# The first norm of a two-block transformer kernel: its loads get places of their own, and its script goes by quarters

## The chip, the cores and the metric

The kernel runs on one core of one Trainium2 chip. The metric is the device time of one execution in microseconds (us); lower is better.

## The reference

Two transformer blocks run one after the other on 256 tokens of 1024 features. The change touches only the beginning of the first block: the modulation vector from the condition `c`, the first norm with its shift and scale, and the first columns of the input projection that follow it.

```python
def first_block(x, c, w_ada, b_ada, norm1_pre, ...):
    ada = jax.nn.silu(c) @ w_ada[l] + b_ada[l]            # 6 x 1024 values
    sh1, sc1, g1, sh2, sc2, g2 = jnp.split(ada, 6, axis=-1)
    h = modulate(rms_norm(x, norm1_pre[l]), sh1, sc1)     # norm * (1 + sc1) + sh1
    y = token_mixer(h, w_in[l], ...)                      # begins with h @ w_in
    x = x + g1[:, None, :] * rms_norm(y, norm1_post[l])
    ...                                                   # expert layer, second block
```

## The kernel before

Activations lie with features on the 128 partitions: 1024 features are eight groups (k = 0 to 7) of 128 rows by 256 tokens. Weights come in slabs of 128 by 1024 float32 (512 KB, one load each). Each projection slab is split into a high part (`whi`, ScalarE, line 315) and a low part (`wlo`, VectorE or, for a few listed slabs, GpSimd, line 323), and the activations likewise (`h[0]`, `h[1]`); a product of a slab and a feature group is three matmuls, high by high, high by low, low by high (lines 404 to 406). Slabs 3 and 4 of `w_qk` are among those whose low part GpSimd makes.

The start of `mixer` follows two lists that were written by hand. Every engine works through its own instructions in the order in which the program issues them, and all loads of this part are issued by SyncE, in one queue.

`LOADS` is the order of the loads. `x0`, `x1` are the two halves of the input; `w1` to `w5` the first five slabs of `w_qk`; `S0` to `S7` the eight slabs of `w_sh`, which hold the columns of `w_ada` for the shift; `c0` to `c7` the eight slabs of `w_ada` for the scale, transposed. The slabs S and c go through `pieces`: `ask` issues their loads into tiles of a pool (here `mraw`, four buffers), `piece` takes the next one and computes with it.

`START` is the order of the work. A name that is in `LOADS` means: take all pieces up to this one. For S that is four matmuls into one row of 256 values, eight instructions in the trace (`shift`, line 746): two S slabs give 256 shift values, a quarter of the features. For c it is a dot product on VectorE with the row `crow`, the condition on all partitions (`dot`, lines 522 and 523). The other names are steps: `q` squares of half the input and their column sums (lines 778 and 571), `R` the reciprocal root, `B` its spread over the partitions (line 576), `X` a quarter of the normed input (line 789), `H` the transposes that turn a quarter of the shift from a row into columns (lines 793 to 797), `u` the use of the next weight slab, with its split, `h` and `l` the modulated feature group and its split (lines 818, 681, 683, 400), `P` all products that have become possible and are not done.

`crow` is made on TensorE: eight broadcasts of the condition's columns (line 576), and two copies by ScalarE (line 765). The tiles of the pool `sp` (the pool `mix`) have one buffer for each tag: a tile that names a tag takes over the buffer of the earlier tile of that tag.

When the script is done, the kernel loads five more weight slabs, appends the other 32 units of the modulation to `pieces` (they are taken one at a time during the following projections), and goes on with `w_if`, the rest of `w_qk`, `w_v` and so on.

Of the kernel before, what the change touches and what calls it, by code (L numbers as in the profile page):

```python
# [11 lines left out]
F32 = mybir.dt.float32  # L12
# [5 lines left out]
AF = mybir.ActivationFunctionType  # L18
# [3 lines left out]
P = 128  # L22
T = 256
D = 1024
KC = 8
# [4 lines left out]

START_SLABS = 5
START_LOADS = 4
LOADS = (
    "S0 x0 x1 S1 S2 w1 S3 S4 w2 w3 S5 w4 w5 S6 c0 S7 c1 c2 c3 c4 c5 c6 c7"
).split()
START = (
    "S0 q0 q1 S1 H0 R0 S2 B0 X0 X1 X2 X3 S3 u0 S4 u1 S5 u2 H2 u3 P0 H1 S6 c0 h0 S7 c1 l0 u4 H3 h1 c2 l1 "
    "h2 P1 c3 l2 h3 P2 c4 l3 h4 c5 l4 P3 P4 h5 c6 l5 P5 h6 c7 l6 P6 h7 l7 P7"  # L40
).split()

POOL_FFN = [5, 7, 9]
# [7 lines left out]
OFF, HALF = 4, 8  # L51
# [83 lines left out]
def _outsT(w):  # L135

    return np.ascontiguousarray(w.T).reshape(-1, P, D)
# [8 lines left out]
def _layout(i):  # L146
    o = {}
    o["cols"], offs = _cols(i)
    o["xT"] = np.ascontiguousarray(i["x"][0].T.reshape(KC, P, T).transpose(1, 0, 2))
    o["crow"] = np.ascontiguousarray(i["c_2"])  # L150
    o["posr"] = np.ascontiguousarray(i["positions_2"].reshape(1, T))
    o["posc"] = np.ascontiguousarray(i["positions_2"].reshape(2, P).T)
    w = i["w_ada"][0]
    o["w_sh"] = np.ascontiguousarray(w[:, :D].reshape(2, 4, P, 4, T).transpose(3, 0, 2, 1, 4)).reshape(-1, P, D)
    o["w_ada"] = _outsT(w[:, D:])
    w = i["w_in"][0]
    o["w_c"], o["w_b"], o["w_x"] = (_blocksT(w[:, j * D:(j + 1) * D]) for j in range(3))
    o["w_qk"] = _blocksT(w[:, 3 * D:4 * D])
# [28 lines left out]
    r = uq[:, :, 128:]  # L187
# [80 lines left out]
class Body:  # L268
# [236 lines left out]
    def crow_of(self, pool):  # L505

        c = pool.tile([P, D], F32, name="crow1")
        self.nc.sync.dma_start(c, self.a["crow"].broadcast_to([P, D]))
        return c

    def silu_row(self, c, e):
# [125 lines left out]
        self.nc.sync.dma_start(self.x[:, s], self.a["xT"][:, s])  # L637

    def ada_u(self, units):
        self.add_cols(lambda u: self.a["w_ada"][u - KC], self.ada, self.colr("b_ada", 0, 48), units)  # L640

    def mod_u(self, l, units):
        self.add_cols(lambda u: self.a[f"mod{l}"][u - (ROW_UNITS if l == 0 else 0)], self.mod[l], self.colr("mod_b", 48 * l, 48), units)
# [77 lines left out]
    def mixer(self):  # L721
        nc, a = self.nc, self.a
        with ExitStack() as ctx:
            self.tmps = ctx.enter_context(self.pool_l("tmps1", 14))
            sp = ctx.enter_context(self.pool_l("mix", 1))
            self.mctx = ExitStack()
            mp = self.mctx.enter_context(self.pool_r("mraw", 4))
# [3 lines left out]
            x = self.x  # L731

            c8 = self.cp.tile([P, KC], F32, name="c8")
# [5 lines left out]
            def shift(n):  # L739
                q, b = divmod(n, 2)  # L740

                def take(raw):
                    if b == 0:
                        v[q] = self.pst()
                    for k in range(4):
                        nc.tensor.matmul(v[q][0:1, :T], c8[:, 4 * b + k:4 * b + k + 1], raw[:, k * T:(k + 1) * T],
                                         start=b == 0 and k == 0, stop=b == 1 and k == 3)
                return take

            for w in LOADS:  # L750
                n = int(w[1])
                if w[0] == "S":
                    self.pieces.append((a["w_sh"][n], shift(n)))
                elif w[0] == "c":
                    self.ada_u([KC + n])
                else:
                    self.pieces.append(({"x": lambda n=n: self.load_x(n), "w": lambda n=n: self.load(n)}[w[0]], None))
            self.cap, self.hold = START_SLABS, 1
            self.pieces_in(mp, START_LOADS)
            self.crow = sp.tile([P, D], F32, name="crow0")  # L760
            for n in range(2):
                pt = self.pst()
                for k in range(4):
                    self.bcast(pt[:, k * P:(k + 1) * P], c8[:, 4 * n + k:4 * n + k + 1])
                nc.scalar.activation(self.crow[:, n * 512:(n + 1) * 512], pt, AF.Copy)
            st = self.pst()
            xn = f8("xn", "qk")
            a1 = self.cp.tile([P, KC], F32, name="a1")
            h = act8("h")
# [1 line left out]
            pair = [sp.tile([P, 2 * D + HALF], F32R, name="w3" + m, tag="ya" + m)[:, :2 * D].rearrange("p (a t) -> p a t", t=D) for m in "hl"]  # L771
            for n in range(3, START_SLABS):
                self.spare[n] = [t[:, n - 3] for t in pair]

            def sums(n):
                for kc in range(4 * n, 4 * n + 4):
                    sq = self.tmp("sq")
                    nc.scalar.activation(sq, x[:, kc], AF.Square)
                    self.colstat(st, sq, 0, kc == 0)
# [37 lines left out]
            def high(k):  # L817
# [4 lines left out]
                         u=lambda j: ws.append(self.use(("w_qk", j, 0, D))))  # L822
            left = list(LOADS)
            for w in START:
                if w in left:
                    n = left.index(w) + 1
# [4 lines left out]
            self.cap = 9999  # L831
            self.load(START_SLABS + self.RAW)
            self.ada_u(range(16, 48))
            self.hold = 0


            qk = f8("qk")
# [23 lines left out]
            self.after()  # L861
            for j in range(START_SLABS):
                self.spawn(g_qk(pts[j]))
# [49 lines left out]

            for j in range(START_SLABS, 8):
                self.block("w_qk", j, h, g_qk)
# [3 lines left out]
            vs = sp.tile([P, 2, D], F32, name="vs")  # L919
# [3 lines left out]
            so = f8("so")  # L923
# [9 lines left out]
            hm = f8("hm")  # L933
# [102 lines left out]
            sga, sgm = f8("sga"), f8("sgm")  # L1036
# [39 lines left out]
            st = self.pst()  # L1076
# [1001 lines left out]
```

## Time and profile before

| what | value |
|---|---|
| median of 3 runs | 1741.29 us (1740.84 to 1745.04) |
| profiled execution | 1745.1 us, its span in the trace 1743.0 us |
| TensorE busy | 1710.9 us, 98% of the span |
| VectorE, ScalarE, GpSimd busy | 1381.6, 1037.9, 218.1 us |
| bytes moved | 371.17 MB, 213 GB/s on average |

The span is the time from the first to the last instruction of the profiled execution; the device time of the same execution has 2.1 us around it. Busy times of TensorE count matmuls that run into each other, and "granted clock" (PEclk) is the clock of TensorE as a share of 2.4 GHz.

### The profile page before, as it was taken

The page shows a single profiled execution, that of the slowest core. Times are in us where ns is not written, and L with a number is a line of the kernel's source. Part 1 is how long each engine was busy: PE and PEld are TensorE (multiplying, and loading weights), DVE is VectorE, ACT ScalarE, POOL GpSimd, SP SyncE. Part 2 cuts the span into 40 slices and gives each one's busy share as a digit, 9 for nine tenths or more (in the row PEclk, how much of TensorE's full clock was granted, in tenths as well). Part 3 has the DMA queues.
Part 4 walks back from the last instruction along what each step waited for, and adds up shares of the span by engine and source line. Part 5 has one row for each costly group of instructions (what it writes and reads, how often), then busy time and mean ns, then how long its engine had stood idle before and what let it go on. Part 6 is the DMA issues. An engine that isn't in the chain of part 4 may idle for free.

```text
span 1743.0 us, 33343 instructions
## 1 busy us (share of the span) xinstructions
PE 1710.9 (98%) x12720; PEld 1594.2 (91%) x12720; DVE 1381.6 (79%) x2845; ACT 1037.9 (60%) x1910; POOL 218.1 (13%) x235
## 2 busy tenths in 40 slices
PE   8999999999999999999999999999999999999997
PEld 5899999799999999998888888888999998999997
DVE  4778778589988889987878888876799867688754
ACT  3764544455555999975544555555676547567543
POOL 1110100000010876540000000030200000020001
PEclk8999999999999999999999999999999999999999
DMA  8676677555555544447888888852367664436562
GB/s 291 249 255 217 218 255 248 187 170 182 194 182 183 165 162 159 161 155 276 301 312 297 291 304 299 291 187 98 126 233 289 235 254 159 156 123 217 183 182 72
DMA packets 102400, 371.17 MB, mean 213 GB/s; under 512 B 11456, under 2 KB 11968, under 8 KB 101856
## 3 DMA queue, kind: packets, MB, share of 16 engines
q1 hardware_dynamic: 101664, 365.76, 61.2%
q0 software_dynamic: 576, 3.29, 0.5%
q8 instruction: 99, 1.62, 0.4%
q14 instruction: 61, 0.50, 0.1%
HBM read 365.99 MB, written 2.10 MB: 211 GB/s over the span
## 4 chain that ended last, share of the span: by engine, by line
PE 88%; DVE 4%; ACT 3%; DMA 2%; issue 2%; POOL 1%; POOLq 0%; ACTq 0%; DVEq 0%; SPq 0%
PE ps L404 20%; PE ps L406 19%; PE ps L405 19%; PE ps L1282 5%; PE ps L1281 5%; PE ps L1283 5%; DMA wraw<-v 2%; PE ps L1210 2%; PE ps L571 1%; DVE wlo L323 1%; PE ps L451 1%; PE ps L452 1%; PE ps L453 1%; PE ps L476 1%; PE ps L478 1%
## 5 line engine op out<-in xcount | busy, mean ns | idle before, releaser
L315 ACT ACTIVATE whi<-wraw 128x1024 fp32r<-128x1024 f32 (+1 forms) x548 | 574.1, 1050 | 450.4 <-PE ps L405 191.7
L323 DVE TENSOR_TENSOR wlo<-wraw,whi 128x1024 fp32r<-128x1024 f32 (+1 forms) x538 | 650.0, 1212 | 51.2 <-ACT whi L315 50.0
L404 PE MATMUL ps<-h2h,whi 128*128 128x256 f32 x1152 | 329.8, 286 | 0.0
L406 PE MATMUL ps<-h2h,wlo 128*128 128x256 f32 x1152 | 320.4, 278 | 0.2 <-DVE wlo L323 0.2
L405 PE MATMUL ps<-h2l,whi 128*128 128x256 f32 x1152 | 317.4, 276 | 0.0
L406 PE MATMUL ps<-hhh,wlo 128*128 128x256 f32 x800 | 224.5, 281 | 4.2 <-DVE wlo L323 4.2
L404 PE MATMUL ps<-hhh,whi 128*128 128x256 f32 x800 | 227.4, 284 | 0.9 <-ACT hhh L683 0.8
L405 PE MATMUL ps<-hhl,whi 128*128 128x256 f32 x800 | 224.2, 280 | 1.3 <-DVE hhl L400 1.1
L404 PEld LDWEIGHTS ps<-h2h,whi 128*128 128x128 f32 x1152 | 216.4, 188 | 0.4 <-ACT za L681 0.4
L405 PEld LDWEIGHTS ps<-h2l,whi 128*128 128x128 f32 x1152 | 216.7, 188 | 0.0
L406 PEld LDWEIGHTS ps<-h2h,wlo 128*128 128x128 f32 x1152 | 215.5, 187 | 0.6 <-DVE wlo L323 0.4
L1282 PE MATMUL ps<-whi,al 128*128 128x512 f32 x512 | 199.9, 390 | 0.8 <-DVE al L400 0.8
L1281 PE MATMUL ps<-whi,ah 128*128 128x512 f32 x512 | 199.5, 390 | 0.5 <-ACT ah L1227 0.4
L1283 PE MATMUL ps<-wlo,ah 128*128 128x512 f32 x512 | 199.2, 389 | 0.0
L1202 POOL TENSOR_SCALAR L<-iota,i1T,eT 128x128 bf16<-128x128 f32 x128 | 143.1, 1125 | 270.1 <-DVE mT L1504 136.9
L522 DVE SCALAR_TENSOR_TENSOR mraw<-mraw,crow 128x1024 f32<-128x1024 f32 x128 | 157.1, 1227 | 0.0
L406 PEld LDWEIGHTS ps<-hhh,wlo 128*128 128x128 f32 x800 | 150.1, 188 | 4.8 <-DVE wlo L323 4.8
L404 PEld LDWEIGHTS ps<-hhh,whi 128*128 128x128 f32 x800 | 151.3, 189 | 2.4 <-ACT hhh L683 1.6
L405 PEld LDWEIGHTS ps<-hhl,whi 128*128 128x128 f32 x800 | 150.4, 188 | 2.7 <-DVE hhl L400 2.4
L404 PE MATMUL ps<-hh,whi 128*128 128x256 f32 (+1 forms) x440 | 126.3, 287 | 0.0
L406 PE MATMUL ps<-hh,wlo 128*128 128x256 f32 (+1 forms) x440 | 123.5, 281 | 0.5 <-DVE wlo L323 0.5
L405 PE MATMUL ps<-hl,whi 128*128 128x256 f32 (+1 forms) x440 | 123.0, 279 | 0.0
(461 smaller groups left out, 3509.0 us busy)
## 6 DMA issues: line engine op xcount, KB each, us to landing
wraw<-u SPq DMA_DIRECT2D x128, 512.0 KB, 3.3
wraw<-v SPq DMA_DIRECT2D x128, 512.0 KB, 5.9
mraw<-mod SPq DMA_DIRECT2D x88, 512.0 KB, 4.2
wraw<-fa SPq DMA_DIRECT2D x44, 512.0 KB, 4.2
wraw<-fb SPq DMA_DIRECT2D x44, 512.0 KB, 4.4
mraw<-w_ada SPq DMA_DIRECT2D x40, 512.0 KB, 4.0
wraw<-fo SPq DMA_DIRECT2D x32, 512.0 KB, 4.4
wraw<-wq SPq DMA_DIRECT2D x16, 512.0 KB, 3.6
```

Source lines behind the costliest of these rows:

```text
L315: nc.scalar.activation(t[:, :hi - lo], self.raws[self.n_hi][:, :hi - lo], AF.Copy)
L323: e.tensor_tensor(t[:, :n], self.raws[self.n_lo][:, :n], self.his[self.n_lo].bitcast(F32)[:, :n], ALU.subtract)
L404: mm(out, lh, rh, start=start, stop=False, **kw)
L405: mm(out, lh, rl, start=False, stop=False, **kw)
L406: mm(out, ll, rh, start=False, stop=stop, **kw)
L451: mm(pts[tt][hf], ah, wh[:, s], start=kc == 0, stop=False)
L522: nc.vector.scalar_tensor_tensor(raw, raw, 1.0, self.crow, op0=ALU.mult, op1=ALU.mult, accum_out=acc)
L1202: nc.gpsimd.tensor_scalar(L[:, k], iota, i1, e, op0=ALU.is_equal, op1=ALU.mult)
L1210: nc.tensor.matmul(pg[:, k * P:(k + 1) * P], L[:, k], half[:, k, h], start=h == 1, stop=h == 0)
L1281: mm(o, ah, w[0][:, s], start=first, stop=False)
L1282: mm(o, al, w[0][:, s], start=False, stop=False)
L1283: mm(o, ah, w[1][:, s], start=False, stop=last)
```

## The change

The condition's row is loaded from HBM (`crow0`, to all partitions) and its sigmoid product made there by ScalarE and VectorE; the broadcasts on TensorE go. Of the shift, features 0 to 5 stay with TensorE (six slabs S); features 6 and 7 become dot products like the scale (`s6`, `s7`). All loads of the start are asked for at once, into tiles under the tags of seven later tensors, then the pool `mraw`. `START` is ordered by quarters of the features. After the script, four more slabs of `w_ada` are asked for at once.

```diff
--- before.py
+++ after.py
@@ -30,14 +30,15 @@
 
 
 
+
 START_SLABS = 5
-START_LOADS = 4
+SHIFT_PE = 6
 LOADS = (
-    "S0 x0 x1 S1 S2 w1 S3 S4 w2 w3 S5 w4 w5 S6 c0 S7 c1 c2 c3 c4 c5 c6 c7"
+    "r0 x0 x1 c0 S0 S1 c1 w1 S2 c2 S3 c3 w2 S4 c4 S5 c5 w3 s6 c6 w4 s7 c7 w5"
 ).split()
 START = (
-    "S0 q0 q1 S1 H0 R0 S2 B0 X0 X1 X2 X3 S3 u0 S4 u1 S5 u2 H2 u3 P0 H1 S6 c0 h0 S7 c1 l0 u4 H3 h1 c2 l1 "
-    "h2 P1 c3 l2 h3 P2 c4 l3 h4 c5 l4 P3 P4 h5 c6 l5 P5 h6 c7 l6 P6 h7 l7 P7"
+    "q0 q1 c0 R0 S0 B0 X0 S1 c1 X1 H0 u0 h0 X2 h1 l0 S2 l1 P0 c2 S3 H1 X3 h2 c3 h3 l2 u1 l3 P1 S4 c4 S5 H2 h4 c5 l4 h5 u2 l5 P2 "
+    "s6 c6 h6 l6 u3 s7 P3 c7 h7 u4 l7 P4"
 ).split()
 
 POOL_FFN = [5, 7, 9]
@@ -147,12 +148,13 @@
     o = {}
     o["cols"], offs = _cols(i)
     o["xT"] = np.ascontiguousarray(i["x"][0].T.reshape(KC, P, T).transpose(1, 0, 2))
-    o["crow"] = np.ascontiguousarray(i["c_2"])
+    o["crow0"], o["crow1"] = np.ascontiguousarray(i["c"]), np.ascontiguousarray(i["c_2"])
     o["posr"] = np.ascontiguousarray(i["positions_2"].reshape(1, T))
     o["posc"] = np.ascontiguousarray(i["positions_2"].reshape(2, P).T)
     w = i["w_ada"][0]
-    o["w_sh"] = np.ascontiguousarray(w[:, :D].reshape(2, 4, P, 4, T).transpose(3, 0, 2, 1, 4)).reshape(-1, P, D)
-    o["w_ada"] = _outsT(w[:, D:])
+    n = SHIFT_PE * P
+    o["w_sh"] = np.ascontiguousarray(w[:, :n].reshape(2, 4, P, n // T, T).transpose(3, 0, 2, 1, 4)).reshape(-1, P, D)
+    o["w_ada"] = _outsT(w[:, n:])
     w = i["w_in"][0]
     o["w_c"], o["w_b"], o["w_x"] = (_blocksT(w[:, j * D:(j + 1) * D]) for j in range(3))
     o["w_qk"] = _blocksT(w[:, 3 * D:4 * D])
@@ -505,7 +507,7 @@
     def crow_of(self, pool):
 
         c = pool.tile([P, D], F32, name="crow1")
-        self.nc.sync.dma_start(c, self.a["crow"].broadcast_to([P, D]))
+        self.nc.sync.dma_start(c, self.a["crow1"].broadcast_to([P, D]))
         return c
 
     def silu_row(self, c, e):
@@ -637,7 +639,7 @@
         self.nc.sync.dma_start(self.x[:, s], self.a["xT"][:, s])
 
     def ada_u(self, units):
-        self.add_cols(lambda u: self.a["w_ada"][u - KC], self.ada, self.colr("b_ada", 0, 48), units)
+        self.add_cols(lambda u: self.a["w_ada"][u - SHIFT_PE], self.ada, self.colr("b_ada", 0, 48), units)
 
     def mod_u(self, l, units):
         self.add_cols(lambda u: self.a[f"mod{l}"][u - (ROW_UNITS if l == 0 else 0)], self.mod[l], self.colr("mod_b", 48 * l, 48), units)
@@ -747,23 +749,7 @@
                                          start=b == 0 and k == 0, stop=b == 1 and k == 3)
                 return take
 
-            for w in LOADS:
-                n = int(w[1])
-                if w[0] == "S":
-                    self.pieces.append((a["w_sh"][n], shift(n)))
-                elif w[0] == "c":
-                    self.ada_u([KC + n])
-                else:
-                    self.pieces.append(({"x": lambda n=n: self.load_x(n), "w": lambda n=n: self.load(n)}[w[0]], None))
-            self.cap, self.hold = START_SLABS, 1
-            self.pieces_in(mp, START_LOADS)
             self.crow = sp.tile([P, D], F32, name="crow0")
-            for n in range(2):
-                pt = self.pst()
-                for k in range(4):
-                    self.bcast(pt[:, k * P:(k + 1) * P], c8[:, 4 * n + k:4 * n + k + 1])
-                nc.scalar.activation(self.crow[:, n * 512:(n + 1) * 512], pt, AF.Copy)
-            st = self.pst()
             xn = f8("xn", "qk")
             a1 = self.cp.tile([P, KC], F32, name="a1")
             h = act8("h")
@@ -771,6 +757,36 @@
             pair = [sp.tile([P, 2 * D + HALF], F32R, name="w3" + m, tag="ya" + m)[:, :2 * D].rearrange("p (a t) -> p a t", t=D) for m in "hl"]
             for n in range(3, START_SLABS):
                 self.spare[n] = [t[:, n - 3] for t in pair]
+
+            def row():
+                nc.sync.dma_start(self.crow, a["crow0"].broadcast_to([P, D]))
+
+            for w in LOADS:
+                n = int(w[1])
+                if w[0] == "S":
+                    self.pieces.append((a["w_sh"][n], shift(n)))
+                elif w[0] in "sc":
+                    self.ada_u([n + (KC if w[0] == "c" else 0)])
+                else:
+                    self.pieces.append(({"r": row, "x": lambda n=n: self.load_x(n), "w": lambda n=n: self.load(n)}[w[0]], None))
+            self.cap, self.hold = START_SLABS, 1
+
+            later = [(sp.tile([P, 2, D], F32, name="early" + n, tag=n), k) for n in ("sga", "sgm", "hm", "so", "vs") for k in range(2)]
+            later += [(sp.tile([P, 2 * D + HALF], F32, name="early" + n, tag=n)[:, :2 * D].rearrange("p (a t) -> p a t", t=D), k)
+                      for n in ("ymh", "yml") for k in range(2)]
+            later = [t[:, k] for t, k in later]
+
+            class Early:
+
+
+                def tile(self, *args, **kwargs):
+                    return later.pop(0) if later else mp.tile(*args, **kwargs)
+
+            self.mpool, self.mdepth = Early(), 0
+            self.ask(99)
+            self.mpool, self.mdepth = mp, 0
+            self.silu_row(self.crow, sp.tile([P, 2, D], F32, name="esig", tag="qk")[:, 0])
+            st = self.pst()
 
             def sums(n):
                 for kc in range(4 * n, 4 * n + 4):
@@ -831,6 +847,8 @@
             self.cap = 9999
             self.load(START_SLABS + self.RAW)
             self.ada_u(range(16, 48))
+            self.mdepth = 4
+            self.ask(4)
             self.hold = 0
```

## Rows read from the trace of the kernel before

**Rows 1.** The page's first part: engines' busy time and share of the span.

```profile
PE 1710.9 (98%) x12720; PEld 1594.2 (91%) x12720; DVE 1381.6 (79%) x2845; ACT 1037.9 (60%) x1910; POOL 218.1 (13%) x235
```

**Rows 2.** Stretches of the start: length, busy time (instructions) by engine, PEclk, DMA share, GB/s.

```profile
8.00:16.00 8.00, 7.60 (x47) 4.70 (x45) 0.00 (x0) 3.03 (x11) 0.00 (x0) 0.88 1.02 414
...
14.00:20.00 6.00, 5.54 (x17) 2.02 (x14) 0.23 (x2) 3.21 (x4) 0.70 (x1) 0.50 0.91 339
...
30.00:35.00 5.00, 3.22 (x17) 1.51 (x15) 3.50 (x8) 2.23 (x4) 1.41 (x2) 0.95 0.54 168
...
34.70:38.10 3.40, 3.40 (x17) 3.38 (x18) 3.00 (x8) 1.02 (x2) 1.90 (x2) 0.53 0.94 372
```

**Rows 3.** Timeline of SyncE's queue, 0 to 60 us.

```profile
...
2.59 0.95 SPq L543 DMA_DIRECT2D mraw<-w_sh  x2
...
26.67 12.94 SPq L543 DMA_DIRECT2D mraw<-w_ada  x7
39.66 0.42 SPq L346 DMA_DIRECT2D wraw<-w_if  x1
...
```

**Rows 4.** Waits of SyncE's queue, 0 to 120 us: total, times, longest.

```profile
SPq L543 <- DVE ada L523: 39.3, 11, 5.6
...
SPq L543 <- PE ps L746: 17.7, 6, 4.8
```

**Rows 5.** Loads of mraw, landings from 3, 20 and 26 us on; u.

```profile
L543 SPq DMA_DIRECT2D mraw<-w_sh x3: 432/481/683, 2.6 to 4.2; - x3
...
DMA to landing us min/median/max: 7.3/8.1/9.6
...
L543 SPq DMA_DIRECT2D mraw<-w_ada x1: 328/328/328, 23.2 to 23.2; - x1
...
DMA to landing us min/median/max: 4.2/4.3/4.4
...
DMA to landing us min/median/max: 3.8/4.8/6.5
...
wraw<-u SPq DMA_DIRECT2D x128, 512.0 KB, 3.3
```

**Rows 6.** Timeline of the start: TensorE.

```profile
4.08 3.52 PE L576 MATMUL ps<-ident,c 128*128 128x128 f32 x16 [4.08 <-DVE c L735]
...
17.00 3.57 PE L746 MATMUL ps<-mraw,c 128*1 128x256 f32 x8
...
20.50 0.87 PE L576 MATMUL ps<-ident,rr 128*128 128x128 f32 x4
...
21.30 5.34 PE L746 MATMUL ps<-mraw,c 128*1 128x256 f32 x24
...
27.11 0.60 PE L796 MATMUL ps<-ones,t_shr 1*128 1x1 f32 x4 [0.46 <-ACT t_shr L793]
```

**Rows 7.** Timeline of the start: other engines; last a group of VectorE.

```profile
26.96 1.04 ACT L315 ACTIVATE w3h<-wraw 128x1024 fp32r<-128x1024 f32 x1
...
28.08 2.34 POOL L323 TENSOR_TENSOR w3l<-wraw,w3h 128x1024 fp32r<-128x1024 f32 x1 [9.89 <-ACT w3h L315]
...
29.03 2.47 DVE L522 SCALAR_TENSOR_TENSOR mraw<-mraw,crow 128x1024 f32<-128x1024 f32 x1
...
36.29 1.21 DVE L522 SCALAR_TENSOR_TENSOR mraw<-mraw,crow 128x1024 f32<-128x1024 f32 x1
...
36.41 0.60 ACT L681 ACTIVATE t_nh<-xn,ada,a 128x256 f32<-128x256 f32 x1 [2.22 <-DVE a L818]
...
37.04 0.42 ACT L683 ACTIVATE hh<-t_nh 128x256 fp32r<-128x256 f32 x1
...
L323 DVE TENSOR_TENSOR wlo<-wraw,whi 128x1024 fp32r<-128x1024 f32 x4 | 4.7, 1219 | 0.5 <-ACT whi L315 0.5
```

**Rows 8.** Timeline of TensorE: first product, first of the next block.

```profile
34.96 0.58 PE L404 MATMUL ps<-hh,whi 128*128 128x256 f32 x1
...
50.52 0.28 PE L404 MATMUL ps<-hh,whi 128*40 128x256 f32 x1
```

## The prediction

> **What bounds the kernel now.** I read the page first, then the stretches of the start, SyncE's queue, the landings of the loads, and the timeline of each engine up to the first projection. Over the span TensorE is busy 98% [rows 1], so nothing can be won from the long phases without taking TensorE work away, and the change takes none away there. The exception is the start. Until 34.96 TensorE has no projection product to do, the first one starts at that moment and the first product of the next block (w_if) at 50.52 [rows 8]: 120 products (five slabs, eight features, three each) in 15.6 us, and from there on the kernel follows TensorE. So the price of this change is one number: how much earlier or later than 50.5 the last of these 120 products ends. The work behind it is the same in both kernels, moves along with it, and its next long wait (the gate chain, which starts from w_if's end) moves too.
>
> The start itself is a chain of loads, vector work and short TensorE bursts. With several loads queued the stream runs at 414 GB/s with the DMA engines full (1.02) [rows 2], that is 1.27 us for a slab of 524,288 bytes; but in the start most slabs are not queued early. Seven slabs of w_ada take 12.94 us to issue, because each waits for a buffer, and the load of w_if, behind them in the same queue, starts only at 39.66 [rows 3]. What they wait for is in the queue's own waits: a load that takes a buffer over waits until the last reader of the tile before it has finished, a dot product on VectorE (39.3 us in 11 waits) or a shift slab on TensorE (17.7 us in 6) [rows 4]. A load that meets a nearly empty queue then needs 4.2 to 4.4 us to land (3.8 at the least over the later ones) [rows 5].
>
> **The change, part by part.**
>
> *The places.* The new pool `later` calls `sp.tile` once for every pair of a tag and a half k, in a pool with one buffer for each tag. That makes two tiles on one buffer, not one tile with two halves. As with the buffers of `mraw` [rows 4], the second tile's load waits for the last reader of the first, although it writes the other half. The order of the loads then gives the pairs c0|S0, S1|c1, S2|c2, S3|c3, S4|c4, S5|c5, s6|c6; only s7 and c7 (from the pool of four), the five weight slabs, x and the condition row are free of it. As all of them stand in one queue on SyncE, each of the seven waits also holds every load behind it. So the change, as I read it, does not queue 23 loads: it puts seven trips "use, then issue, then land" one behind the other. For such a trip I take 4.2 us [rows 5], for each load queued right behind it 1.27 more. Bounds: 3.3 (the expert slabs' median) and 4.8 (the median of the later w_ada loads) [rows 5].
>
> The Trainium skill, DMA: Bandwidth & Descriptors, in its anatomy of one DMA, fits 2.0 us plus the bytes over 436 GB/s for loads issued on the GpSimd path; as an estimate that is 3.2 us for a slab where the trace shows 4.2, and by it the seven trips would be 7.0 us shorter in all and the time near 1778.
>
> *The durations.* A shift slab is 1.78 us on TensorE at 2.4 GHz (5.34 for three) and 3.57 at 1.2; the spread of the norm 0.87; the transposes of a quarter 0.60 [rows 6]. A dot product is 1.21 to its buffer's release and about 1.4 with its addition; the affine 0.60 and its high part 0.42; a slab's high part 1.04, its low part 1.22 on VectorE and 2.34 on GpSimd (slabs 3 and 4), during which a dot product that starts takes 2.47 instead of 1.21 [rows 7]. A product triple is 0.35 (15.6 us over 40, less the first few at the low clock).
>
> *Turn by turn, TensorE at 2.4 GHz.* c0 is the fourth big load, in the place that S1 has now (issued 2.59 or soon after, landing 7.3 later) [rows 3, 5]: 9.9. Its dot ends at 11.1; the condition row, the first load, and its sigmoid and product are done before that. S0 is issued at 11.1 and lands at 15.3, S1 at 16.6.
> Turn 2: S0 to 17.1, the spread of the norm to 18.0, S1 to 19.8; c1 lands at 24.0, w1 25.3, S2 26.6.
> Turn 3: S2 to 28.4; c2 lands 32.6, S3 33.9 (the first products, P0, fit in between).
> Turn 4: S3 to 35.7; c3 lands 39.9, w2 41.2, S4 42.4. On TensorE S4 stands behind P1, and P1 needs c3's dot (41.3), feature 3 (42.5), slab 1's high part (43.5, behind it on ScalarE) and low part (44.7); its last five triples end at 46.6.
> Turn 5: S4 to 48.4; c4 lands 52.6, S5 53.8.
> Turn 6: S5 to 55.6; c5 lands 59.8, w3 61.1, s6 62.4. VectorE takes s6 only behind c5's dot, feature 5 (62.8), slab 2's high (63.8) and low part (65.0) and l5: s6's dot ends at 66.6.
> Turn 7: c6 lands 70.8, w4 72.1, s7 73.3, c7 74.6, w5 75.9. Feature 6 at 73.4, slab 3's high part 74.5, its low part on GpSimd to 76.8, which holds c7's dot until then: 78.1. Feature 7 at 79.5, slab 4's high part 80.5, its low part on GpSimd 82.9, and behind it nearly all of P4, twelve triples: **86.9**.
>
> *The clock.* The granted clock was 0.50 from 14 to 20, after the one-column sums of the squares, and 0.53 from 34.7 to 38.1, after a stretch in which TensorE worked 3.22 us of 5 [rows 2]. The new start is sparser: between two bursts TensorE waits 4 us or more for a load. At 1.2 GHz each of the six shift slabs, all on the chain, costs 1.78 more, the spread 0.9, P1 about 1.8 and P4 up to 4: between 0 and 17. I take four slabs, 7.1, as most bursts follow a wait: the end comes at **94.0**, 43.5 later than now.
>
> *What costs nothing.* The eight broadcasts of the condition and two copies go away (3.5 us of TensorE from 4.08 on [rows 6]); the first shift slab waits for its load far longer, so they save nothing. The condition row is one load more, 1.27 us, and its sigmoid and product lie before c0's landing; if that cover went, c0's dot would be late by at most 1 us. Shift slabs 6 and 7 become two dot products: s6 is counted above, s7 lies beside slab 3. `ask(4)` issues four w_ada slabs behind the five weight loads: w_v0 is issued when slab 4's low part frees its place, as now, some 11 us before its product, so the four add about 5 us to a queue with that slack. w_if and w_qk 5 and 6 come earlier in relation to their use, which TensorE, full at that point, can't turn into time.
>
> *Sum.* The profiled execution took 1745.1 with a span of 1743.0; 1745.1 + 43.5 = 1788.6. It lies 3.8 above the median of the runs (1741.3), so in the median's terms **1785**. Bounds: trips of 3.3 and the high clock throughout end at 80.6 (+30, 1771); trips of 4.8 and the low clock throughout at 108 (+58, 1799).
>
> **The rivals.** *The places are places of their own after all* (the change does what it says): for it speaks that the halves don't overlap, against it that buffers are handed over whole [rows 4]. Then the loads stream at 1.27 each from c0's 9.9, and the last, w5, lands at 35.2. But the engines still work in the order written. P0 ends near 21, S3 behind it 22.9, the transposes 24.1, c3's dot 26.0, feature 3 27.3, slab 1 high and low 29.6, P1 31.5; only then S4 and S5 (35.1), though both landed by 25.1; transposes 36.3, c5's dot 37.6, feature 5 39.3, slab 2 41.5, P2 44.6; feature 6 45.8, slab 3 49.2 on GpSimd, c7's dot 50.4, feature 7 51.8, slab 4 55.2, P4 59.2. That is 8.7 later than now at the high clock and up to 9 more at the low: 1750 to 1759, I take 1755. The kernel before had its shift complete and its weights split by 35 and then ran one dense stretch; the new order gives up that density for products that start early and wait.
>
> *Faster:* places of their own, and the quarters keep up with the loads, so that the end hangs on the last load alone: 35.2 + 1.04 + 2.34 + 4.1 = 42.7, 7.8 earlier, 1733. It decides from the point where P1 ends before S5 lands (25.1); against it stands the queue of TensorE above, 6 us late there.
> The Trainium skill, DMA: Bandwidth & Descriptors, under bandwidth, holds that HBM binds a core's loads at about 358 GB/s; the 414 of the trace is above that, and by 358 this rival's last load would come 4 us later, for a time near 1737.
>
> **How the numbers follow.** Paired places 0.86; own places but slower 0.09; nearly no change 0.03 (own places, half of the 8.7 hidden); faster 0.02. What a measurement can tell from no change is about 0.3%, 5 us. Slower 0.95, same 0.03, faster 0.02. The paired case's own range is 1771 to 1799; as its unknown, the clock, weighs on one side only, I set 1766 to 1798, which leaves out the own-place cases (0.14) and a small part of the paired one.
>
> **What would show it.** In the new trace: SyncE's loads waiting seven times, on c0's and s6's dots and on five shift slabs; stretches of 4 us between 10 and 70 with TensorE and VectorE idle and the DMA engines mostly empty; the first product before 34.96 but w_if's first product near 94; the clock at 1.2 GHz in several of the gaps; the rest of the kernel as before, moved. I am wrong if the loads of c0 to w5 are issued back to back before 15 us (then the rivals hold), or if w_if starts below 80 or above 108.

## The result and the profile after

The kernel after takes **1787.53 us** (median of 5 runs, 1783.82 to 1790.65) where the kernel before took 1741.86 beside it (5 runs, 1740.84 to 1745.04): a ratio of **1.0248**, 95% interval 1.0229 to 1.0267. It is slower by 45.7 us. The forecast was 1785, range 1766 to 1798.

The page's first part, after: TensorE's busy time has grown by 4 us only [rows 1], while the span has grown from 1743.0 to 1785.2.

```profile
PE 1714.8 (96%) x12684; PEld 1596.5 (89%) x12684; DVE 1386.3 (78%) x2851; ACT 1036.8 (58%) x1908; POOL 219.5 (12%) x235
```

SyncE's queue, after (start, length, line, load), where before one long run of loads stood [rows 3]:

```profile
2.58 0.63 SPq L545 DMA_DIRECT2D earlysga<-w_ada  x1
12.45 0.33 SPq L545 DMA_DIRECT2D earlysga<-w_sh  x1
...
22.30 0.33 SPq L545 DMA_DIRECT2D earlysgm<-w_ada  x1
...
32.34 0.33 SPq L545 DMA_DIRECT2D earlyhm<-w_ada  x1
...
40.58 0.33 SPq L545 DMA_DIRECT2D earlyso<-w_ada  x1
...
55.25 0.33 SPq L545 DMA_DIRECT2D earlyvs<-w_ada  x1
...
63.66 0.33 SPq L545 DMA_DIRECT2D earlyymh<-w_ada  x1
...
64.51 9.55 SPq L545 DMA_DIRECT2D earlyyml<-w_ada  x2
...
76.09 0.48 SPq L348 DMA_DIRECT2D wraw<-w_if  x1
```

The waits of that queue up to 120 us (waited for: total, times, longest), to be held against [rows 4]:

```profile
SPq L545 <- PE ps L748: 23.6, 5, 8.5
SPq L545 <- DVE ada L525: 18.3, 2, 9.4
```

Every second load into a tag (`earlysga`, `earlysgm` and so on) is issued 8 to 14 us after the first. Seven waits stand there, five on the products of a shift slab (S1 to S5) and two on the addition behind a dot product (c0, s6). These are the seven pairs.

Stretches of 10 us, after (columns as in [rows 2]):

```profile
20.00:30.00 10.00, 4.13 (x20) 1.73 (x20) 4.69 (x10) 2.03 (x3) 0.00 (x0) 0.82 0.43 157
...
50.00:60.00 10.00, 5.21 (x23) 3.36 (x21) 0.84 (x1) 0.00 (x0) 0.00 (x0) 0.81 0.32 107
60.00:70.00 10.00, 3.93 (x12) 1.32 (x12) 2.57 (x10) 2.38 (x6) 0.00 (x0) 0.70 0.43 157
```

No engine is full, and the DMA engines are 57 to 68% empty. What the loads cost here is not the stream's rate but the time of one trip, from issue to landing.

TensorE's timeline, after; the answer to [rows 6, 8]:

```profile
16.28 3.53 PE L748 MATMUL ps<-earlysga,c 128*1 128x256 f32 x8 [0.19 <-DVE rv L590]
...
28.73 3.57 PE L748 MATMUL ps<-earlyhm,c 128*1 128x256 f32 x8 [5.41 <-DMA earlyhm<-w_sh]
...
37.28 3.27 PE L748 MATMUL ps<-earlyso,c 128*1 128x256 f32 x8 [3.61 <-DMA earlyso<-w_sh]
...
47.96 0.58 PE L406 MATMUL ps<-hh,whi 128*128 128x256 f32 x1 [6.35 <-ACT whi L317]
...
60.30 3.33 PE L748 MATMUL ps<-earlyymh,c 128*1 128x256 f32 x8 [5.09 <-DMA earlyymh<-w_sh]
...
71.02 0.58 PE L406 MATMUL ps<-hh,whi 128*128 128x256 f32 x1 [6.32 <-ACT whi L317]
...
93.91 0.28 PE L406 MATMUL ps<-hh,whi 128*40 128x256 f32 x1
```

The first product of `w_if` has moved from 50.52 to 93.91, by 43.4 us; the span has grown by 42.2. So the whole loss lies in the start. From here on I give that moment for each kernel. It is the sharper measure: from it to the end of the span the traces take 1688.0 to 1699.1 us (`e12_noask`, which changes that part, excepted), so one span carries some 5 us either way that have nothing to do with the start. It comes from a single trace of each kernel, though, and is good to about 1 us: `e12_noask`, whose start is that of `e1_own`, has 69.73 for 69.39, and inside these two starts the same steps lie up to 1.0 us apart.

Loads up to 76 us, after (size, time from issue to landing, the median where there are several):

```profile
crow<-crow SPq DMA_DIRECT2D x1, 512.0 KB, 5.0
earlysga<-w_ada SPq DMA_DIRECT2D x1, 512.0 KB, 8.5
earlysga<-w_sh SPq DMA_DIRECT2D x1, 512.0 KB, 3.7
...
earlysgm<-w_ada SPq DMA_DIRECT2D x1, 512.0 KB, 3.2
...
earlyvs<-w_ada SPq DMA_DIRECT2D x1, 512.0 KB, 3.8
```

### The profile page after: what moved, and what is told of

Same layout as the page of the kernel before. It is cut to its first block, busy times and chain, and to the rows that moved or that the text cites. A ratio compares the mean times of both kernels' runs of the same rounds, so it can differ in the third digit from the quotient of the medians.

```text
span 1785.2 us, 33274 instructions
## 1 busy us (share of the span) xinstructions
PE 1714.8 (96%) x12684; PEld 1596.5 (89%) x12684; DVE 1386.3 (78%) x2851; ACT 1036.8 (58%) x1908; POOL 219.5 (12%) x235
## 4 chain that ended last, share of the span: by engine, by line
PE 87%; DVE 5%; ACT 3%; DMA 3%; issue 1%; POOL 1%; SPq 0%; POOLq 0%; ACTq 0%; DVEq 0%
PE ps L406 19%; PE ps L408 18%; PE ps L407 18%; PE ps L1300 6%; PE ps L1301 6%; PE ps L1299 6%; PE ps L1228 2%; PE ps L573 1%; PE ps L748 1%; DVE wlo L325 1%; PE ps L453 1%; PE ps L454 1%; PE ps L455 1%; PE ps L478 1%; PE ps L480 1%
## 5 line engine op out<-in xcount | busy, mean ns | idle before, releaser
L524 DVE SCALAR_TENSOR_TENSOR mraw<-mraw,crow 128x1024 f32<-128x1024 f32 x122 | 148.6, 1218 | 0.0
```

The lines of the kernel that those rows point to most:

```text
L524: nc.vector.scalar_tensor_tensor(raw, raw, 1.0, self.crow, op0=ALU.mult, op1=ALU.mult, accum_out=acc)
```

## The experiments

Each was timed beside the kernel before, whose median was 1743.5 to 1745.1 us in these comparisons; ratios are to it. The kernel after stands at 1.0248, 93.91.

| kernel | time, us | ratio (95%) | `w_if`'s first product, us |
|---|---|---|---|
| e1_own | 1767.10 | 1.0118 (1.0094 to 1.0142) | 69.39 |
| e6_onepair | 1768.81 | 1.0142 (1.0125 to 1.0159) | 74.86 |
| e4_warm | 1789.66 | 1.0255 (1.0227 to 1.0283) | 93.77 |
| e5_warm2 | 1783.44 | 1.0230 (1.0211 to 1.0249) | 89.59 |
| e8_ownwarm | 1760.29 | 1.0101 (1.0084 to 1.0118) | 65.19 |
| e7_pecrow | 1763.69 | 1.0117 (1.0100 to 1.0133) | 68.23 |
| e10_order | 1759.66 | 1.0084 (1.0060 to 1.0108) | 65.98 |
| e11_eight | 1770.58 | 1.0145 (1.0118 to 1.0172) | 75.85 |
| e12_noask | 1802.66 | 1.0343 (1.0316 to 1.0369) | 69.73 |
| e2_oldscript | 1744.94 | 1.0001 (0.9984 to 1.0019) | 53.36 |
| e3_best | 1743.33 | 0.9996 (0.9978 to 1.0014) | 48.47 |
| e9_bestwarm | 1741.83 | 0.9987 (0.9973 to 1.0001) | 46.76 |

**e1_own.** The kernel after, with one whole tile for each tag, whose halves are handed out.

```diff
-            later = [(sp.tile([P, 2, D], F32, name="early" + n, tag=n), k) for n in (...) for k in range(2)]
+            for n in ("sga", "sgm", "hm", "so", "vs"):
+                t = sp.tile([P, 2, D], F32, name="early" + n, tag=n)
+                later += [t[:, k] for k in range(2)]
...                                        # the same for "ymh" and "yml"
```

> The changed kernel with one tile for each of the seven tags, its two halves handed out separately, so that no load of the start shares a tile with another; order and all else as changed. Paired tiles as the cause: all 24 loads are issued before 15 us, none waits for a dot product or a shift slab, the last lands near 36, and about 25 us of the 45 come back. The order written into the script then costs the rest: w_if's first product between 60 and 70 (now 93.9), time 1752 to 1763, still slower than before. Rival, the order by quarters alone is the cause (the loads would have been late anyway): within 5 us of 1787. Rival, the order is good and only the pairs spoil it: w_if's first product before 50, time below 1740.

Nothing else differs, and 24.5 of the 43.4 us are gone (93.91 to 69.39). The time, 1767, is above the 1752 to 1763 expected. No load of the pairs waits for a dot or a slab any more. From 8.4 us on they are issued one every 1.28 us or so, the last, w5, at 26.29, and not all before 15 as I had expected. Stretches of e1_own:

```profile
20.00:30.00 10.00, 8.45 (x37) 3.54 (x36) 6.86 (x15) 3.25 (x6) 0.00 (x0) 1.00 1.03 410
...
40.00:50.00 10.00, 5.45 (x25) 2.45 (x24) 2.05 (x8) 3.35 (x6) 0.00 (x0) 0.84 0.01 2
```

The loads now stream at 410 GB/s until they are all there, by 40 the DMA engines are idle (share 0.01), and TensorE still works only half the time. Its timeline says why:

```profile
35.75 0.58 PE L406 MATMUL ps<-hh,whi 128*128 128x256 f32 x1 [4.47 <-ACT whi L317]
...
40.72 2.31 PE L748 MATMUL ps<-earlyvs,c 128*1 128x256 f32 x8
...
69.39 0.28 PE L406 MATMUL ps<-hh,whi 128*40 128x256 f32 x1
```

S4 (`earlyvs`) had long landed, but in TensorE's order it stands behind the second products, and these wait for the high part of w2. The pairs are the larger cause, not the only one: 18.9 us are left.

**e6_onepair.** e1_own with one pair put back, S4 and c4.

```diff
+                if n == "vs":
+                    later += [sp.tile([P, 2, D], F32, name="early" + n, tag=n)[:, k] for k in range(2)]
+                    continue
```

> The kernel with a place of its own for each load, but with one pair put back: S4 and c4 share one place. Theory (each pair costs one trip of a load, since it holds everything behind it in SyncE's queue): c4 is issued only after S4's last product, near 43 us in place of 14.8, and S5, c5 and the rest 1.3 us apart behind it; S5 runs near 48 for 42.9, and w_if's first product moves from 69.4 to 72 to 76, the time from 1767 to 1769 to 1773 us. Rival (one pair is covered by the work that the order of steps makes late anyway): first product within 1 us of 69.4 and time 1766 to 1768. If all seven pairs cost alike, one is 24.5 us over 7, or 3.5 us.

SyncE's queue holds c4 from 13.7 to 42.17, with all loads behind it:

```profile
13.32 0.33 SPq L545 DMA_DIRECT2D earlyvs<-w_sh  x1
42.17 0.33 SPq L545 DMA_DIRECT2D earlyvs<-w_ada  x1
```

and on TensorE S5 comes at 46.73 for 42.87, after 4.59 us of idling for its load, at the low clock:

```profile
46.73 3.08 PE L748 MATMUL ps<-earlyymh,c 128*1 128x256 f32 x8 [4.59 <-DMA earlyymh<-w_sh]
```

One pair costs 5.5 us at `w_if`; that is more than a seventh of the 24.5 (3.5), so pairs are not equal or don't simply add up. In the time it can't be told from e1_own (the intervals overlap).

**e4_warm and e5_warm2.** The kernel after, with matmuls that nobody reads in TensorE's idle stretches, to hold the clock. They differ in how many there are (51 broadcasts in e4, 167 in e5) and in a few of the places; the edit shown is that of e5.

```diff
-    "q0 q1 c0 R0 S0 B0 X0 S1 c1 X1 H0 u0 h0 X2 h1 l0 S2 l1 P0 c2 S3 H1 X3 h2 ... P1 S4 c4 S5 H2 h4 ... s7 P3 ..."
+    "F9 q0 F12 q1 c0 R0 S0 B0 X0 S1 c1 X1 F8 H0 F18 u0 h0 X2 h1 l0 S2 l1 P0 F20 c2 S3 F4 H1 F28 X3 h2 ... P1 S4 c4 F22 S5 H2 F28 h4 ... s7 F18 P3 ..."
+            def filler(*digits):      # F9: nine broadcasts, two matmuls each
+                ...
+                        self.bcast(pt[:, k * P:(k + 1) * P], c8[:, k:k + 1])
```

> The changed kernel (paired tiles kept) with extra matmuls on TensorE that compute nothing used, put where it waits for loads: about 51 broadcasts of 128 columns in groups before the column sums, the transposes, the third, fourth and sixth shift slab and the second products. If the low clock costs about 7 us or more on the chain, the shift slabs fall towards 1.78 us and w_if's first product comes 4 to 8 us earlier than 93.9: 1780 to 1784. If the clock is not on the chain (the loads' trips hide it), no gain or a loss of up to 5 us by the added work.

> The changed kernel with its pairs, and fp32 broadcasts whose results nobody reads put into TensorE's idle stretches ahead of the second statistics, S1, S2, S3, the second products, S4, S5, the third products and the fourth, about twice as many as in the kernel before this one, so that each stretch is filled until the load lands. Theory (the pairs set seven trips, and on top of them TensorE's low clock lengthens the slabs and products that stand on the chain): the six shift slabs take 1.9 us each, 11 to 13 us together for the 17.9 of the changed kernel; the second and third products take about 2.9 and 3.4 us for 4.9 and 7; w_if's first product comes at 82 to 88 in place of 93.9, and the time is 1774 to 1783 us. Rival (the clock lies beside the loads' trips and costs nothing): first product at 92 to 94, time 1786 to 1789. If the fillers run longer than the gaps, each overshoot delays its slab by at most 1 to 2 us, and the first product comes between the two.

In e4_warm the fillers were too few: each of their matmuls took 0.13 us at the high clock, so that they ended 2.5 to 3.3 us before S2, S3, S5 and the second products could start, and S0, S2, S3 and S5 still took 2.9 to 3.3 us; it says little on the clock. In e5_warm2 all six slabs ran at 2.4 GHz (matmuls of S2 and S5: least, median, greatest ns):

```profile
L747 PE MATMUL ps<-earlyhm,c x8: 377/379/380, 29.5 to 31.0; 128*1 128x256 f32 x8
...
L747 PE MATMUL ps<-earlyymh,c x8: 377/378/379, 56.9 to 58.4; 128*1 128x256 f32 x8
```

The six slabs take 11.3 us together for 17.9, 6.6 less, but `w_if` comes only 4.3 us sooner, short of the 6 to 12 that I expected. The time, 1783.4 for 1787.5, points the same way, with overlapping intervals. Two things ate the rest. The fillers between the halves of the statistics overshot: S0, issued 0.8 sooner, was used at 18.49 for 16.28, and c1 was issued at 22.87 for 22.30.

```profile
18.49 1.89 PE L747 MATMUL ps<-earlysga,c 128*1 128x256 f32 x8
```

And the last turn didn't shorten (from c6's issue to `w_if` 20.8 us for 20.2): it hangs on VectorE, ScalarE and GpSimd. So 4.3 is what holding the clock gave back less what the fillers cost, and not the clock's whole price.

**e8_ownwarm.** The same fillers in e1_own (`F9`, `F3` at the statistics, `F18` before the second and the third products).

> The kernel with a place of its own for each load, with fp32 broadcasts that nobody reads ahead of the statistics, of the second products (18) and of the third (18). Theory (of the 19 us by which its first product of w_if still lies behind the kernel before, a part is TensorE at 1.2 GHz): statistics 3.7 us for 7.0, second products 2.9 for 5, third 3.4 for 6.4; w_if's first product at 62 to 66 for 69.4, time 1759 to 1764 us. Rival (the order of the steps on VectorE and ScalarE sets the products' starts, and TensorE's rate lies inside its waits): first product at 68 to 70, time 1766 to 1768.

4.2 us sooner than e1_own. The fillers didn't reach everything: half of the sums (3.41 us for 1.84 in e5_warm2), S0 (3.35 for 1.89) and some six triples of the fourth products (0.64 for 0.35 each) still ran at 1.2 GHz. By these numbers I estimate 4.8 us at most that the clock can still hold here, so at least about half of the 18.9 us is not the clock.

**e7_pecrow.** e1_own with the condition row made by TensorE's broadcasts, without its load.

```diff
-    "r0 x0 x1 c0 ...
+    "x0 x1 c0 ...
-            self.silu_row(self.crow, ...)
+            for n in range(2):
+                pt = self.pst()
+                for k in range(4):
+                    self.bcast(pt[:, k * P:(k + 1) * P], c8[:, 4 * n + k:4 * n + k + 1])
+                nc.scalar.activation(self.crow[:, n * 512:(n + 1) * 512], pt, AF.Copy)
```

> The kernel with a place of its own for each load, but with the condition row made on TensorE by the eight broadcasts of the kernel before and two ScalarE copies, and without its load. Theory of the prediction (the row's load costs nothing, since its 512 KB lie beside other loads): first product of w_if within 1 us of 69.4, time 1766 to 1769. Rival (the row's load delays x by about 1.3 us, and its absence on TensorE leaves the statistics at 1.2 GHz, 7.0 us for 3.7): the first shift slab starts near 12.5 for 15.8, and w_if's first product comes at 66 to 68, time 1763 to 1766.

1.2 us sooner, just over the 1 us of "nothing". The two halves of x land 5.0 us after their issue for 7.1 (medians), but TensorE makes the row until 8.2, ScalarE copies it until 8.8 and squares x only then, and the statistics still ran at 1.2 GHz (6.95 us); the first slab starts at 16.18 for 15.82. So the rival's reason was wrong. Nor is the 1.2 us the load's: the spread (0.71 us for 1.22), S1 (1.89 for 2.20) and S4 (1.89 for 2.31) ran at a higher clock here, and S5 begins at 41.73 for 42.87. In e12_noask, which does load the row, the same happens, and S5 begins at 41.83. "Nothing" holds as far as these traces can tell.

**e10_order.** e1_own with S4, S5 and their columns ahead of the second products, and in the loads S5 ahead of c4.

```diff
-... S4 c4 S5 c5 ...
+... S4 S5 c4 c5 ...
...
-... X3 h2 c3 h3 l2 u1 l3 P1 S4 c4 S5 H2 h4 c5 ...
+... X3 h2 c3 S4 S5 H2 h3 l2 u1 l3 P1 c4 h4 c5 ...
```

> The kernel with a place of its own for each load, with one thing moved in the order: the slabs S4 and S5 and their shift columns stand ahead of the second products, and S4, S5 ahead of c4, c5 in the loads. Theory (what is left behind the kernel before is the order: S4 and S5 had landed by 30 us, and stood in TensorE's queue behind products that waited for ScalarE's upper part of w2): the fifth and sixth blocks' dots and affines start when VectorE is free, near 38, the third products near 43 to 45 for 49.9, and w_if's first product comes at 62 to 65 for 69.4; time 1759 to 1763 us. Rival (the sixth and later blocks are set by VectorE's dots and the lower parts of the weights, which this doesn't move): first product at 68 to 70, time 1766 to 1768.

3.4 us sooner than e1_own; the third products begin at 46.27 for 49.91. The direction is that of the theory, and the time (1759.7) lies in its range; `w_if` is just short of the 62 to 65 expected. S3 fell to the low clock here (3.35 us for 1.89), though TensorE's order is unchanged up to it, so the move may be worth up to 1.5 us more. The profiled execution was the slowest of the four (1766.89, the others 1758.64 to 1759.84). From 40 to 50 VectorE is busy 7.80 of 10 us; it may be the next limit, which no run tests.

**e11_eight.** e1_own with the last quarter of the shift as two slabs on TensorE again.

```diff
-SHIFT_PE = 6
+SHIFT_PE = 8
...                                        # and S6, S7 for s6, s7 in LOADS
-    "s6 c6 h6 l6 u3 s7 P3 c7 h7 u4 l7 P4"
+    "S6 c6 S7 H3 h6 l6 u3 P3 c7 h7 u4 l7 P4"
```

> The kernel with a place of its own for each load, with the last quarter of the shift back on TensorE: eight shift slabs, no s6 and s7 as dots on VectorE. Theory of the prediction (the quarter as dots costs nothing, two dots of 1.2 us taking the place of two slabs and the columns): first product of w_if within 1 us of 69.4, time 1766 to 1769. Rival (two dots more on VectorE in the stretch in which GpSimd takes w3's lower parts hold up the last blocks): first product 2 to 4 us sooner, 65.5 to 67.5, time 1763 to 1766. The other way (two slabs at 1.2 GHz of 3.5 us each and their copies are dearer than two dots): first product at 71 to 74, time 1768 to 1772.

6.5 us later, more than any branch of the expectation. TensorE's timeline:

```profile
55.74 1.89 PE L748 MATMUL ps<-earlyyml,c 128*1 128x256 f32 x8
57.47 1.89 PE L748 MATMUL ps<-mraw,c 128*1 128x256 f32 x8
...
62.77 0.38 PE L406 MATMUL ps<-hh,w3h 128*128 128x256 f32 x1 [2.35 <-ACT w3h L317]
```

The slabs themselves are quick (1.9 us each); but they stand behind the third products in TensorE's order, so their feature group begins at 60.5 for 54.2 (its scale on VectorE). As dot products they had run on VectorE beside those products. In this order the dots are worth 6.5 us; in one that has the slabs earlier they need not be.

**e12_noask.** e1_own without the two lines behind the script.

```diff
-            self.mdepth = 4
-            self.ask(4)
```

> The kernel with a place of its own for each load, without the two lines behind the first norm that ask for four adaLN slabs at once; they are asked for later, as in the kernel before. Theory of the prediction (these four loads cost nothing: nobody waits for them early, and no weight is held up behind them): first product of w_if within 1 us of 69.4 and time 1765 to 1769 us. Rival (the four slabs, 2.1 us of issues near 66 and 5 us of transfers, hold up the w_v slabs behind them): time 2 to 4 us less, 1763 to 1765. The other way (the slabs are then late for the dots that feed the next modulation): 2 to 4 us more, 1769 to 1771.

All three branches missed: +35.6 us on e1_own (the medians), and `w_if` where it was (69.73). VectorE's waits from 80 to 500 us:

```profile
DVE mraw L524 <- DMA mraw<-w_ada: 64.4, 26, 4.8
```

I had read the lines as four early loads. They set the depth to which `ask` loads ahead, which the start has set to 0. Without them each later dot product issues its own load and waits for it, 26 times up to 500 us. In the change they only restore what the kernel before had.

**e2_oldscript and e3_best.** e2: the kernel before, its two lists kept, only with its loads issued at once into places of their own. e3: own places, six slabs and two dots, the row on TensorE, and both lists rewritten so that loads, VectorE and TensorE stay dense.

```diff
e2:
-            self.pieces_in(mp, START_LOADS)
...                                        # places as in e1_own
+            self.mpool, self.mdepth = Early(), 0
+            self.ask(99)
+            self.mpool, self.mdepth = mp, 4
e3:
...                                        # places and row as in e7_pecrow
+    "x0 x1 S2 w1 S4 w2 S5 c1 w3 c2 w4 S3 c5 s6 S0 c3 S1 c4 w5 c0 s7 c6 c7"
+    "S2 q0 P0 S4 q1 u0 S5 R0 c1 u1 B0 c2 X1 H2 X2 P2 S3 c5 s6 P3 u2 u3 H1 S0 h5 c3 h3 S1 l5 h2 X0 c4 l3 l2 H0 ..."
```

> The kernel before with one part of the change alone, and that as it was meant: all 23 loads asked for at once into places of their own (one tile for each tag); the old lists LOADS and START, the eight shift slabs and the condition row made on TensorE stay. If the start before was held by loads that came late, w_if's first product moves from 50.5 to 45 or earlier, 1736 or less. If it was held by the order of the engines' own work (my theory: TensorE took shift slabs without a gap from 21 to 27, and the first product waited for the last transposes and the low part of slab 4), it moves by less than 2 us: 1739 to 1744, and the dot products start earlier without effect.

> Places of their own, features 6 and 7 of the shift as dot products, the condition row made on TensorE again, and a script in which the shift slabs of all quarters, the weight splits and the dot products are spread so that no engine stands at a wait while another of its steps could run. If the price of the order is what is left once the pairs are gone, this order is worth more than the old one: w_if's first product at 44 to 47, time 1736 to 1739 (0.2 to 0.35% below before). If the order does not matter, it falls where the kernel of own places and the changed order falls.

e2 shows that early loads alone bring nothing: by 38 nothing is left to load (DMA share 0.00 from 38 to 40), and `w_if` comes 2.8 us later than before. The clock accounts for these 2.8: TensorE's first slab, the sums and the second slab, first before and then in e2:

```profile
7.52 1.89 PE L746 MATMUL ps<-mraw,c 128*1 128x256 f32 x8
9.34 3.73 PE L571 MATMUL ps<-ones,t_sq 128*128 128x1 f32 x32
13.00 2.60 PE L746 MATMUL ps<-mraw,c 128*1 128x256 f32 x8
```

```profile
7.76 2.83 PE L746 MATMUL ps<-earlysga,c 128*1 128x256 f32 x8
10.52 4.65 PE L571 MATMUL ps<-ones,t_sq 128*128 128x1 f32 x32
15.10 3.57 PE L746 MATMUL ps<-earlysga,c 128*1 128x256 f32 x8
```

They take 2.83 us more together. So the loads of the start before did not bind it: with all of them early, nothing is gained, and nothing is lost but the clock. e3 is 2.1 us sooner than before at `w_if`, short of what I expected, and its time can't be told from that of the kernel before.

**e9_bestwarm.** e3_best with `F14` before `H0`, where TensorE idled 3.7 us.

> The kernel with own places and a rewritten order of loads and steps, with 14 broadcasts that nobody reads ahead of the shift columns of the first quarter, in the 3.7 us in which TensorE stood idle before 32.16. Theory (the first 15 products after that gap ran at 1.2 GHz, 0.21 us for 0.12): w_if's first product at 46.5 to 47.5 for 48.47, and the time 1 to 2 us under that kernel's, 1740 to 1743 us, or 0.998 to 1.000 of the kernel before. Rival (products wait on VectorE's dots and lower parts, so a faster TensorE only waits longer): first product at 48 to 48.6. A version that beats the kernel before by over 0.3% isn't expected by either.

`w_if` comes at 46.76, 1.7 us sooner, and the ratio is 0.9987 (0.9973 to 1.0001). The fillers did lift the products behind `H0` to the high clock, but most of the 1.7 us is older than they are. The second half of the sums, e3 and then e9:

```profile
15.90 1.95 PE L572 MATMUL ps<-ones,t_sq 128*128 128x1 f32 x16
```

```profile
14.44 1.95 PE L572 MATMUL ps<-ones,t_sq 128*128 128x1 f32 x16
```

That is 1.5 us sooner, 13 us ahead of the fillers, where the two kernels are the same: the first loads landed sooner in this trace. VectorE still has this lead when the fillers begin (its dot with `earlyvs` starts at 26.76 for 28.21). What is left for `F14` is some 0.2 us, so the rival of the expectation, that products wait for VectorE, fits better than the theory. Stretches of e9_bestwarm:

```profile
20.00:30.00 10.00, 8.44 (x51) 4.81 (x50) 9.83 (x23) 3.43 (x8) 2.35 (x1) 1.00 1.02 408
30.00:40.00 10.00, 9.93 (x82) 9.67 (x82) 9.79 (x25) 4.76 (x10) 2.85 (x2) 1.00 0.85 317
```

VectorE is busy 19.6 of these 20 us: with loads, order and clock put right, VectorE looks like the limit; no run takes work from it. This is the best version found, and it is not shown to be faster than the kernel before.

## Why the prediction was right, step by step

**The pairs.** Shown: five waits on slabs, two on dots, in the order named, and e1_own, which takes away nothing else, gives 24.5 us back. The other 18.9 us stay in e1_own. They belong to the clock, as far as it was measured, and by what is left to the order; the turn-by-turn sum contained both without naming them apart. (With the condition row the list has 24 loads, not 23; nothing hangs on that.)

**The turns.** Issue of each pair's second load, us:

| | S0 | c1 | c2 | c3 | c4 | c5 | c6 | `w_if`'s product |
|---|---|---|---|---|---|---|---|---|
| forecast at 2.4 GHz | 11.1 | 19.8 | 28.4 | 35.7 | 48.4 | 55.6 | 66.6 | 86.9 |
| measured | 12.45 | 22.30 | 32.34 | 40.58 | 55.25 | 63.66 | 73.7 | 93.91 |
| difference | 1.4 | 2.5 | 3.9 | 4.9 | 6.9 | 8.1 | 7.1 | 7.0 |

The sum, 94.0 with the clock's 7.1, was met to 0.1 us, and this is partly luck. The lone loads took 3.2 to 3.8 us, not 4.2: seven trips are 24.8 us in place of 29.4, 4.6 too many in the sum. Against that stood what I had left out: c0 landed at 11.1 and not at 9.9, behind the row and x; and the second products, which stand ahead of S4, ran at 1.2 GHz, which the bounds held and the term did not: S4 began 12.4 us after c3's issue, where the sum had 10.9. The rest is spread over the turns. The sums of squares took 6.96 us, not the 3.73 of before, after TensorE had done nothing until 9.1, but that cost nothing: they ended at 16.09, when S0's load, issued at 12.45, was just landing (3.7 us).

The Trainium skill, DMA: Bandwidth & Descriptors, anatomy of one DMA, has a fit for loads on the GpSimd path that gives, as an estimate, 3.2 us for such a slab. The measured 3.2 to 3.8, on SyncE's queue, lie nearer to it than to the 4.2 that I took from [rows 5].

**The clock.** The slabs grew by 7.2 us (17.9 for six at 1.78), the size of the term, and it is four slabs, S0, S2, S3 and S5, that took 3.3 to 3.6 us, as the term assumed. In the trace these 7.2 us lie on the chain, since each pair's second load behind a slab is issued as the slab ends. Holding the clock gave 4.3 us with the pairs, where the fillers delayed S0 by 2.2, and 4.2 without them, where part of the start stayed at 1.2 GHz. These runs are lower bounds, good to the 1 us of a single trace, and no run has the whole start at the high clock.

**What costs nothing.** The row's load: without it the first slab starts no sooner (16.18 for 15.82). Shift slabs 6 and 7 as dots: a gain of 6.5 us in this order, which I had not seen; c7's dot was held up by GpSimd as forecast. VectorE and then GpSimd, after:

```profile
81.56 2.17 DVE L525 TENSOR_TENSOR ada<-macc,cols 128x1 f32<-128x1 f32 x1
```

```profile
80.95 2.77 POOL L325 TENSOR_TENSOR w3l<-wraw,w3h 128x1024 fp32r<-128x1024 f32 x1 [63.81 <-ACT w3h L317]
```

The Trainium skill, SBUF — State Buffer, in "Who interferes with whom", says that a VectorE instruction with two inputs in SBUF is held up by a GpSimd instruction that reads SBUF. The trace agrees: an addition of one column, 0.16 us elsewhere, took 2.17 and ended with GpSimd's subtraction.

`ask(4)`: the four loads cost nothing that shows, but the lines are no addition; they keep the loads ahead that the start had switched off, and are worth 35.6 us.

**The rivals.** "Own places but slow order" is e1_own: right in kind, too small in size (first product at 59.2 to about 68 forecast, 69.4 measured; 1750 to 1759 forecast, 1767 measured). "Faster" named its condition: the second products end before S5 lands. In e1_own S5, issued at 16.05, landed 10.2 us later, and the second products ended near 40.7. The old order has the same answer: in e2_oldscript, with every load there by 38, `w_if` doesn't come sooner. "Nearly no change" needed places of their own too, and with them e1_own still loses 18.9 us.

**What stays open.** Of the 18.9 us between e1_own and the kernel before, part of the clock (4.2) and S4 and S5 behind the second products (3.4) were taken away one at a time. They make 7.6 if they add up, which wasn't tried. Of the other 11 us up to 4.8, the estimate from e8_ownwarm, may still be the clock. I put the rest down to the order by quarters: products that wait for one ScalarE and one VectorE step after the other, and the last two low parts on GpSimd. That is read from the waits, and no run splits it.

## What to carry to other kernels

Before counting prefetched loads, ask which object the framework's buffers are kept by: two tiles under one tag, in a pool with one buffer for each tag, are one buffer, even where they write different halves, and in one in-order queue each such wait holds every load behind it. Early loads gained nothing here where TensorE took its work in an order that made it wait for other engines; read what ends its idle times before moving a load. And a setting that a start switches off (here the depth of loading ahead) has to be counted as a part of the change when it is put back. Last, when a small edit moves a moment of one trace by a microsecond, see whether the trace already differs ahead of the edit.

## What the hardware showed unexpectedly

A full TensorE was not one at the high clock. In e8_ownwarm it was busy in all of the 12 to 18 us, and the granted clock was 0.50, 0.50 and 0.57 there, behind one-column sums (stretches of 2 us):

```profile
12.00:14.00 2.00, 2.00 (x11) 2.00 (x11) 0.24 (x3) 0.00 (x0) 0.00 (x0) 0.50 1.01 414
14.00:16.00 2.00, 2.00 (x8) 1.08 (x9) 0.16 (x1) 0.00 (x0) 0.70 (x1) 0.50 1.04 418
16.00:18.00 2.00, 2.00 (x6) 0.49 (x4) 0.00 (x0) 0.00 (x0) 0.00 (x0) 0.57 1.02 406
```

And the column of the granted clock can mislead at the start of a trace: in e1_own it reads 1.00 from 14 to 20, while S0 takes 3.57 us from 15.82 on, as at 1.2 GHz in [rows 6]. There the durations tell the level.
